# Whole-row gathers in three buffers, products three points later, and blocks of u turned in place, in a decoder layer with a product-key expert layer

## The chip, the cores and the metric

One core of a Trainium2 chip runs the whole layer as one program. The metric is the device time of one execution in microseconds (us). The median of three runs of the kernel before is 3408.37 us (3407.45 to 3411.59).

## What is computed

The reference is one decoder layer over 512 tokens of width 2048, in float32: a modulation from `c`, a projection, a short gated convolution beside differential attention, an output projection, and then a product-key expert layer (PEER). The change lies in that last part:

```python
s1 = jnp.einsum('thd,nd->thn', q[:, :, 0], keys1)      # 8 heads, 128 keys of each half
s2 = jnp.einsum('thd,nd->thn', q[:, :, 1], keys2)
...                                                    # 16 of the 128 x 128 experts per token and head: idx, g
u = jnp.take(expert_u, ib, axis=0)
a = jnp.einsum('thkd,td->thk', u, xb)
w = (jax.nn.gelu(a.astype(jnp.float32), approximate=False) * gb).astype(xb.dtype)
vv = jnp.take(expert_v, ib, axis=0)
return jnp.einsum('thk,thkd->td', w, vv)
```

Each token picks 8 x 16 = 128 of 16384 experts; each expert is a row of 2048 numbers in `expert_u` and one in `expert_v`.

## The kernel before

The kernel is written in a tile language. Its functions emit instructions in program order; a scheduler then gives each engine one fixed order, by simulated times and by dependencies, and no engine leaves that order on the chip. A tile of a pool with `bufs=n` has n buffers, and a new tile waits until an old buffer is free. A dependency called ORDER shapes that order alone; one called SYNC makes the instruction wait on the chip.

**Two ways for the experts.** The first TG = 160 tokens are *gathered*, the other TD = 352 are *dense*. For the dense tokens all 128 blocks of 128 experts are multiplied: `u_block(e)` (L796) makes 48 matmuls of u for a block (L804), a Gelu follows, `w_block(e)` (L829) multiplies by the gates, and `v_group(ch, dg)` (L945) makes the matmuls of v (L960) for a chunk of CH = 8 blocks and a quarter of the columns: 4 steps of 24 matmuls. TensorE works on float32 split into two parts (`split`, L87: ScalarE copies the first part at L88, VectorE subtracts it at L89), three passes for each product.

**Blocks of u.** A block of u must be turned. It lies in `u_dram` in an order in which VectorE's transposes of 32 x 32 finish the turn. `u_turn(n)` (L781) brings half a block: SP loads `ur` (L787, two buffers, a whole block), VectorE transposes one half into `utf` (L792, two buffers), and `split` makes `ut` from it (two buffers). The first NPRE = 12 blocks are turned ahead in `u_ahead` (L533), while TensorE does the output projection: `uar` is loaded, four transposes (L530) write `uat`, and SP stores that in `u_dram`.

**Gathered tokens.** Their rows of u and v come by indirect DMAs that GpSimd issues (`gathered`, L856), half a row (1024 numbers) for each of 128 partitions, into `gt`, four buffers. `gather_u` (L865) multiplies the half row with the token on VectorE and sums it (L867); after all of them `gather_w` applies Gelu and gate; `gather_v` (L876) adds the half row times its weight to `gacc` (L883). Group 0 are 128 tokens with 128 experts each; the other 32 tokens are folded into 32 columns (`gather_next` reloads tokens, indices and gates). That makes 160 x 2 x 2 = 640 gathers and 643 steps.

**Pace.** `pace` collects matmuls: every 12th of a u block, and the last of each 24 in a v group. After each, `gather_to` (L902) emits as many steps as belong there, so that all are emitted at the end of chunk 14; each gather waits (SYNC) for the latest matmul in `pace`, and its product stands right behind it in the program. Blocks 0 to 11 run before the gathers begin.

**Other users of `gt`.** Before that, the four score tiles `held` (L824) and the one-hot tiles `oh` (L920, 88 of them, VectorE at L921), from which TensorE (L930) makes the gate table `g_dram`, take the same four buffers.

**The end.** In the last chunk, `add_gathered(dg)` (L990) transposes the gathered tokens' sums: `ar` from `a_dram` (group 0, L999) and `gacc` (L1003). `store(dg)` (L1011) transposes the result into `ot` (four buffers) and writes it.

Of the kernel before, what the change touches and what calls it, by code (L numbers as in the profile page):

```python
# [39 lines left out]
GBUF = 4  # L40
# [12 lines left out]
PU_BUFS = 1  # L53
# [5 lines left out]
UTF_BUFS = 2  # L59
# [19 lines left out]
def hymba_peer(tc, x, c, positions, w_ada, b_ada, norm1_g, w_in, conv_w, q_norm_g, k_norm_g,  # L79
# [18 lines left out]
    with ExitStack() as ctx:  # L98
# [430 lines left out]
        def u_quarter(t, ur, q):  # L529
            nc.vector.transpose(t, ur[:, :, q * P:(q + 1) * P].rearrange("p b (c r) -> p c b r", r=32))  # L530


        def u_ahead(e):  # L533
            ur = pu.tile([P, 4, 512], F32, name="uar")
            u_load(ur, e)
            t = pu.tile([P, 4, 4, 4, 32], F32, name="uat", bufs=PU_BUFS)
            for q in range(4):
                u_quarter(t[:, q], ur, q)
            nc.sync.dma_start(u_dram[e], t.rearrange("p q c b r -> p (q c b r)"))
# [241 lines left out]
        def u_turn(n):  # L781
            e, q = divmod(n, 2)
            if e >= NK:
                return
            if q == 0:
                UR[0] = up.tile([P, 4, 512], F32, name="ur", bufs=UR_BUFS)
                nc.sync.dma_start(UR[0].rearrange("p b d -> p (b d)"), u_dram[e])  # L787
            if e < NPRE:
                t = UR[0][:, 2 * q:2 * q + 2].rearrange("p a (c b r) -> p (a c) b r", c=4, b=4)
            else:  # L790
                t = up.tile([P, 8, 4, 32], F32, name="utf", bufs=UTF_BUFS)
                nc.vector.transpose(t, UR[0][:, :, q * 256:(q + 1) * 256].rearrange("p b (c r) -> p c b r", r=32))  # L792
            UT[n] = up.tile([P, 2, 8, P], F32R, name="ut", bufs=UT_BUFS)
            split(UT[n], t.rearrange("p c b r -> p c (b r)"))

        def u_block(e, behind=None):  # L796
            pa = psA.tile([P, T], F32, name="pa")
            for q in range(2):
                u_turn(e * 2 + q + AHEAD)
                ut = UT.pop(e * 2 + q)  # L800
                for j in range(8):
                    k = q * 8 + j
                    for n, (a, b) in enumerate(PASSES):
                        mm = nc.tensor.matmul(pa[:, :TD], ut[:, a, j], hd[k][:, b],  # L804
                                              start=(k == 0 and n == 0), stop=(k == KC - 1 and n == 2))
# [18 lines left out]
        held = [scores(qs, i, psV.tile([P, T], F32, name="pv"), gp.tile([P, D // 2], F32, name="gt", bufs=GBUF)[:, 0:T])  # L824
# [29 lines left out]
        ga_a = gp.tile([P, 2, P], F32, name="ga_a")  # L854

        def gathered(src, g, j, f):  # L856
            t = gp.tile([P, D // 2], F32, name="gt", bufs=GBUF)
            d = nc.gpsimd.indirect_dma_start(out=t, out_offset=None, in_=src,  # L858
                                             in_offset=bass.IndirectOffsetOnAxis(ap=gidx[g][:, j:j + 1], axis=0),
                                             element_offset=f * (D // 2))  # L860
# [4 lines left out]
        def gather_u(g, j, f):  # L865
            t = gathered(expert_u, g, j, f)
            nc.vector.scalar_tensor_tensor(t, t, 1.0, h2n[:, f * D // 2:(f + 1) * D // 2], op0=OP.mult, op1=OP.mult,  # L867
                                           accum_out=ga_a[:, f, j:j + 1])

        def gather_w(g, w):  # L870
            a = ga_a[:, 0, :w]
            nc.vector.tensor_tensor(out=a, in0=a, in1=ga_a[:, 1, :w], op=OP.add)
# [3 lines left out]
        def gather_v(g, j, f):  # L876
            t = gathered(expert_v, g, j, f)
            a = ga_a[:, 0, j:j + 1]
            s = slice(f * D // 2, (f + 1) * D // 2)
            if j == 0:  # L880
                nc.vector.tensor_scalar(gacc[:, s], t, a, None, op0=OP.mult)
            else:
                nc.vector.scalar_tensor_tensor(gacc[:, s], t, a, gacc[:, s], op0=OP.mult, op1=OP.add)  # L883
# [10 lines left out]
        for g in range(NG):  # L894
            w = P if g == 0 else P // fold
            if g:
                steps.append((gather_next, ()))
            steps += [(gather_u, (g, j, f)) for j in range(w) for f in range(2)] + [(gather_w, (g, w))] + \
                     [(gather_v, (g, j, f)) for j in range(w) for f in range(2)]
        done = [0]  # L900

        def gather_to(blocks):  # L902
            first = 0.55 * CH
            frac = min(1.0, max(0.0, (blocks - first) / (NK - first - CH)))
            while done[0] < math.ceil(len(steps) * frac):
                f, a = steps[done[0]]
                f(*a)
                done[0] += 1


        with tc.tile_pool(name="gs", bufs=2, side="right") as gs:
# [78 lines left out]
        def add_gathered(dg):  # L990
            if NG == 2:
                ar = fin.tile([P, 512], F32, name="ar")
# [77 lines left out]
```

## Time and profile before

| what | value |
|---|---|
| median of three runs | 3408.37 us |
| the profiled execution's own time | 3427.17 us |
| its span, first to last instruction | 3424.9 us |
| TensorE matmuls busy | 3189.8 us (93%) |
| VectorE busy | 2840.9 us (83%) |
| ScalarE busy | 1219.8 us (36%) |
| GpSimd busy | 1419.2 us (41%) |
| DMA, mean rate | 297 GB/s |
| granted TensorE clock, mean share of full speed | 0.972 |

The engines are PE (TensorE; PEld its weight loads), DVE (VectorE), ACT (ScalarE), POOL (GpSimd) and SP (SyncE, which issues most DMAs). A row names a line of the kernel, an engine and an operation; `out<-in` are the program's tile names. "Idle before" is what the engine stood still just before such instructions, and the arrow names what ended that. Matmuls are pipelined, so that the durations of single ones overlap; a count in a stretch says more than their busy time.

### The profile page before, as it was taken

To read this page: it belongs to the slowest core of one execution; us is meant where nothing else is said; L and a number is where in the kernel's file an instruction comes from. 1 tells how busy PE (TensorE), PEld (TensorE's weight loads), DVE (VectorE), ACT (ScalarE), POOL (GpSimd) and SP (SyncE) were. 2 spreads that over 40 slices of the span, in tenths; PEclk is the share of its full clock that TensorE was granted. 3 is DMA by queue.
4 is the path that set the end of the run, shared out by engine and by line. 5 is a ranking of instruction groups with operands and counts; after the bars stand their busy time and mean duration, and the time that the engine had idled before them with its cause. 6 is when DMAs were issued, how large, how long until landed. Compare 5 with 4: busy or idle time off the path is not lost.

```text
span 3424.9 us, 48472 instructions
## 1 busy us (share of the span) xinstructions
PE 3189.8 (93%) x18006; PEld 2950.5 (86%) x18006; DVE 2840.9 (83%) x4261; ACT 1219.8 (36%) x1826; POOL 1419.2 (41%) x985
## 2 busy tenths in 40 slices
PE   5888999999998869899999999999999999999986
PEld 4666877777877659899899999999999999999985
DVE  5789667842339999889999999989999999999885
ACT  5232344343254437632333332323333333233322
POOL 2446423354436620034454444454444444445441
PEclk9998999999999979999999999999999999999997
DMA  8885978967999789989989999999889898999984
GB/s 292 261 261 173 318 246 279 301 229 223 308 299 299 229 276 342 328 296 340 320 322 334 317 324 315 318 315 336 317 316 333 305 334 317 326 327 331 322 285 174
DMA packets 434987, 1017.92 MB, mean 297 GB/s; under 512 B 34833, under 2 KB 113598, under 8 KB 415166
## 3 DMA queue, kind: packets, MB, share of 16 engines
q1 hardware_dynamic: 342590, 679.23, 58.7%
q0 software_dynamic: 92160, 335.59, 27.4%
q8 instruction: 141, 2.31, 0.3%
q14 instruction: 96, 0.79, 0.1%
HBM read 965.11 MB, written 171.18 MB: 332 GB/s over the span
## 4 chain that ended last, share of the span: by engine, by line
PE 39%; DVE 15%; DMA 11%; issue 6%; POOL 2%; ACT 0%; SPq 0%; DVEq 0%; ACTq 0%; POOLq 0%
PE pa L804 18%; PE pv L960 18%; DMA gt<-in_expert_u_dram,idxu 5%; DVE gt L867 2%; DMA gt<-in_expert_v_dram,ib 2%; PE pv L930 2%; DMA u_dram<-in_expert_u_dram 2%; DVE vs L89 1%; DVE utf L792 1%; DVE ut L89 1%; DVE gt L921 1%; DVE gacc L883 1%; POOL gt L858 1%; DVE tkj L691 1%; PE pm L561 1%
## 5 line engine op out<-in xcount | busy, mean ns | idle before, releaser
L804 PE MATMUL pa<-hd,ut 128*128 128x352 f32 x6144 | 1078.3, 327 | 41.9 <-DVE ut L89 32.3
L960 PE MATMUL pv<-W,vs 128*128 128x352 f32 x6144 | 1058.2, 325 | 20.6 <-ACT W L88 10.1
L804 PEld LDWEIGHTS pa<-hd,ut 128*128 128x128 f32 x6144 | 1010.2, 190 | 48.1 <-DVE ut L89 36.6
L960 PEld LDWEIGHTS pv<-W,vs 128*128 128x128 f32 x6144 | 1004.0, 189 | 26.9 <-ACT W L88 11.9
L89 POOL TENSOR_TENSOR wsp<-wraw,wsp 128x1024 fp32r<-128x1024 f32 x160 | 393.2, 2460 | 546.4 <-ACT wsp L88 519.4
L858 POOL DMA_INDIRECT gt<-in_expert_u_dram,idxu x256 | 347.4, 1357 | 593.8 <-DVE gt L867 239.0
L858 POOL DMA_INDIRECT gt<-in_expert_v_dram,idxu x256 | 342.4, 1337 | 434.9 <-DVE gacc L883 282.5
L88 ACT ACTIVATE vs<-vr 128x1024 fp32r<-128x1024 f32 x256 | 271.4, 1060 | 693.0 <-PE pv L960 635.6
L867 DVE SCALAR_TENSOR_TENSOR gt<-gt,h2n 128x1024 f32<-128x1024 f32 x320 | 384.3, 1217 | 68.7 <-DMA gt<-in_expert_u_dram,idxu 60.4
L883 DVE SCALAR_TENSOR_TENSOR gacc<-gt,ga_a,gacc 128x1024 f32<-128x1024 f32 x316 | 397.8, 1277 | 41.9 <-DMA gt<-in_expert_v_dram,ib 22.6
L88 ACT ACTIVATE ut<-utf 128x1024 fp32r<-128x1024 f32 x232 | 245.2, 1057 | 298.2 <-PE pa L804 184.5
L89 DVE TENSOR_TENSOR vs<-vr,vs 128x1024 fp32r<-128x1024 f32 x256 | 309.7, 1211 | 31.3 <-ACT vs L88 31.3
L88 ACT ACTIVATE wsp<-wraw 128x1024 fp32r<-128x1024 f32 x160 | 169.1, 1058 | 383.8 <-issue 99.7
L89 DVE TENSOR_TENSOR ut<-utf,ut 128x1024 fp32r<-128x1024 f32 x232 | 282.2, 1219 | 22.7 <-ACT ut L88 22.3
L792 DVE STREAM_TRANSPOSE utf<-ur 128x1024 f32<-128x1024 f32 x232 | 287.2, 1240 | 0.1
L471 PE MATMUL pm<-big,wsp 128*128 128x512 f32 x1152 | 284.6, 400 | 0.0
L471 PEld LDWEIGHTS pm<-big,wsp 128*128 128x128 f32 x1152 | 213.9, 190 | 42.4 <-issue 0.2
L196 DVE SCALAR_TENSOR_TENSOR ada_acc<-ada_w,scol,ada_acc 128x512 f32<-128x512 f32 x195 | 201.1, 1031 | 42.5 <-DMA ada_w<-in_w_ada_dram 38.8
L257 PE MATMUL pqk<-wsp,big 128*128 128x512 f32 x768 | 192.4, 409 | 24.7 <-DVE qk L303 17.8
L716 PE MATMUL pm<-big,wsp 128*128 128x512 f32 x768 | 188.8, 404 | 17.0 <-POOL wsp L89 15.4
L257 PEld LDWEIGHTS pqk<-wsp,big 128*128 128x128 f32 x768 | 149.2, 197 | 61.6 <-DVE qk L303 21.5
L716 PEld LDWEIGHTS pm<-big,wsp 128*128 128x128 f32 x768 | 147.1, 195 | 50.1 <-POOL wsp L89 18.0
(274 smaller groups left out, 3197.9 us busy)
## 6 DMA issues: line engine op xcount, KB each, us to landing
ur<-u_dram SPq DMA_DIRECT2D x128, 1024.0 KB, 7.7
vr<-in_expert_v_dram SPq DMA_DIRECT2D x256, 512.0 KB, 6.8
u_dram<-in_expert_u_dram SPq DMA_DIRECT2D x464, 256.0 KB, 6.7
ada_w<-in_w_ada_dram SPq DMA_DIRECT2D x192, 512.0 KB, 5.3
wraw<-in_w_in_dram SPq DMA_DIRECT2D x96, 512.0 KB, 5.9
g_dram<-gtile SPq DMA_DIRECT2D x11, 2048.0 KB, 7.4
g<-g_dram SPq DMA_DIRECT2D x32, 704.0 KB, 9.3
wraw<-in_w_out_dram SPq DMA_DIRECT2D x32, 512.0 KB, 5.5
```

The costliest lines, as they stand in the source:

```text
L88: hi = nc.scalar.activation(dst[:, 0], src, AF.Copy)
L89: (eng or nc.vector).tensor_tensor(out=dst[:, 1], in0=src, in1=dst[:, 0].bitcast(F32), op=OP.subtract)
L196: nc.vector.scalar_tensor_tensor(new, wt[:, k], s, old, op0=OP.mult, op1=OP.add)
L257: nc.tensor.matmul(banks[i], hT[kk][:, a, i * P:(i + 1) * P], ws[:, b, k], start=(kk == last[0] and n == 0), stop=(kk == last[1] and n == 2))
L471: nc.tensor.matmul(banks[n2], ws[:, a, k, n2 * P:(n2 + 1) * P], hT[kk][:, b], start=(kk == 0 and n == 0), stop=(kk == KC - 1 and n == 2))
L716: nc.tensor.matmul(banks[j], ws[:, a, k, j * P:(j + 1) * P], h2T[kk][:, b], start=(kk == 0 and n == 0), stop=(kk == KC - 1 and n == 2))
L792: nc.vector.transpose(t, UR[0][:, :, q * 256:(q + 1) * 256].rearrange("p b (c r) -> p c b r", r=32))
L804: mm = nc.tensor.matmul(pa[:, :TD], ut[:, a, j], hd[k][:, b], start=(k == 0 and n == 0), stop=(k == KC - 1 and n == 2))
L858: d = nc.gpsimd.indirect_dma_start(out=t, out_offset=None, in_=src, in_offset=bass.IndirectOffsetOnAxis(ap=gidx[g][:, j:j + 1], axis=0), e ...
L867: nc.vector.scalar_tensor_tensor(t, t, 1.0, h2n[:, f * D // 2:(f + 1) * D // 2], op0=OP.mult, op1=OP.mult, accum_out=ga_a[:, f, j:j + 1])
L883: nc.vector.scalar_tensor_tensor(gacc[:, s], t, a, gacc[:, s], op0=OP.mult, op1=OP.add)
L960: mm = nc.tensor.matmul(pv[j // 2][:, j % 2, :TD], vs[:, a, bb, j * P:(j + 1) * P], W[e0 // 2][:, m, bb], start=(b == 0 and n == 0), stop= ...
```

## The change

Gathers bring whole rows (2048 numbers), so 320 gathers and 323 steps; `gt` has three buffers of twice the size, and so have the users beside the gathers: `held` needs four of three, and `oh` takes half of one. A product is no longer emitted behind its gather but kept in `held_back` and emitted when `pace` has grown by LAG = 3, or when three are held, or before `gather_w`, `gather_next` and the end. `u_turn` transposes a half of `ur` in place, `utf` is gone, and the split reads `ur` in runs of 32. `u_ahead` transposes `uar` in place, with three buffers, and stores it. `ar` takes a buffer of `ot` instead of two of its own.

```diff
-GBUF = 4
+GBUF = 3
+LAG = 3
-PU_BUFS = 1
+PU_BUFS = 3
-UTF_BUFS = 2
...
         def u_ahead(e):
-            ur = pu.tile([P, 4, 512], F32, name="uar")
+            ur = pu.tile([P, 4, 512], F32, name="uar", bufs=PU_BUFS)
             u_load(ur, e)
-            t = pu.tile([P, 4, 4, 4, 32], F32, name="uat", bufs=PU_BUFS)
-            for q in range(4):
-                u_quarter(t[:, q], ur, q)
-            nc.sync.dma_start(u_dram[e], t.rearrange("p q c b r -> p (q c b r)"))
+            for b in range(4):
+                nc.vector.transpose(ur[:, b], ur[:, b])
+            nc.sync.dma_start(u_dram[e], ur.rearrange("p b d -> p (b d)"))
...
-            if e < NPRE:
-                t = UR[0][:, 2 * q:2 * q + 2].rearrange("p a (c b r) -> p (a c) b r", c=4, b=4)
-            else:
-                t = up.tile([P, 8, 4, 32], F32, name="utf", bufs=UTF_BUFS)
-                nc.vector.transpose(t, UR[0][:, :, q * 256:(q + 1) * 256].rearrange("p b (c r) -> p c b r", r=32))
-            UT[n] = up.tile([P, 2, 8, P], F32R, name="ut", bufs=UT_BUFS)
-            split(UT[n], t.rearrange("p c b r -> p c (b r)"))
+            t = UR[0][:, :, q * 256:(q + 1) * 256]
+            if e >= NPRE:
+                nc.vector.transpose(t, t)
+            UT[n] = up.tile([P, 2, 8, 4, 32], F32R, name="ut", bufs=UT_BUFS)
+            split(UT[n], t.rearrange("p b (c r) -> p c b r", r=32))
...
-        def gathered(src, g, j, f):
-            t = gp.tile([P, D // 2], F32, name="gt", bufs=GBUF)
+        def gathered(src, g, j):
+            t = gp.tile([P, D], F32, name="gt", bufs=GBUF)
             d = nc.gpsimd.indirect_dma_start(out=t, out_offset=None, in_=src,
-                                             in_offset=bass.IndirectOffsetOnAxis(ap=gidx[g][:, j:j + 1], axis=0),
-                                             element_offset=f * (D // 2))
+                                             in_offset=bass.IndirectOffsetOnAxis(ap=gidx[g][:, j:j + 1], axis=0))
...
-        def gather_u(g, j, f):
-            t = gathered(expert_u, g, j, f)
-            nc.vector.scalar_tensor_tensor(t, t, 1.0, h2n[:, f * D // 2:(f + 1) * D // 2], op0=OP.mult, op1=OP.mult,
-                                           accum_out=ga_a[:, f, j:j + 1])
+        def gather_u(g, j):
+            t = gathered(expert_u, g, j)
+            return lambda: nc.vector.scalar_tensor_tensor(t, t, 1.0, h2n, op0=OP.mult, op1=OP.mult,
+                                                          accum_out=ga_a[:, j:j + 1])
...
+        def use_next():
+            i = held_back.pop(0)[1]()
+            if pace:
+                tc.add_manual_dep(i.ins, pace[-1].ins.name, ORDER, reason="rows have landed")
 
         def gather_to(blocks):
             first = 0.55 * CH
             frac = min(1.0, max(0.0, (blocks - first) / (NK - first - CH)))
+            while held_back and held_back[0][0] + LAG <= len(pace):
+                use_next()
             while done[0] < math.ceil(len(steps) * frac):
                 f, a = steps[done[0]]
-                f(*a)
+                while held_back and (len(held_back) == GBUF or f in (gather_w, gather_next)):
+                    use_next()
+                use = f(*a)
+                if use is not None:
+                    held_back.append((len(pace), use))
                 done[0] += 1
+            while held_back and frac == 1.0:
+                use_next()
...
-                    oh = gp.tile([P, D // 2], F32, name="gt", bufs=GBUF).rearrange("p (a t n) -> p a t n", a=2, n=P)
+                    oh = gp.tile([P, D], F32, name="gt", bufs=GBUF)[:, 0:D // 2].rearrange("p (a t n) -> p a t n", a=2, n=P)
...
-                ar = fin.tile([P, 512], F32, name="ar")
+                ar = fin.tile([P, T], F32, name="ot", bufs=4)
```

`gather_v` is changed as `gather_u` is, and `gather_w` no longer adds two half sums.

## Rows read from the trace of the kernel before

**Rows 1.** By stretches: start:end and length, busy us (count) of PE, PEld, DVE, ACT, POOL; clock, DMA share, GB/s.

```profile
1265.00:1380.00 115.00, 110.29 (x810) 109.44 (x809) 108.82 (x140) 86.75 (x200) 0.24 (x1) 0.97 0.90 324
...
1600.00:1720.00 120.00, 112.51 (x676) 110.75 (x676) 111.37 (x145) 35.39 (x40) 57.10 (x44) 0.97 0.91 321
...
1900.00:2320.00 420.00, 408.33 (x2493) 403.78 (x2493) 383.78 (x460) 128.38 (x144) 203.58 (x143) 0.99 0.91 318
2320.00:3000.00 680.00, 680.00 (x4227) 680.00 (x4226) 644.78 (x581) 214.94 (x242) 294.14 (x226) 1.00 0.90 323
...
3302.00:3425.00 123.00, 76.28 (x413) 70.92 (x411) 75.70 (x141) 23.82 (x54) 24.41 (x20) 0.79 0.59 209
```

**Rows 2.** Waits of TensorE, 1900 to 2320: total us, times, longest.

```profile
PE pa L804 <- DVE ut L89: 6.7, 7, 2.3
```

**Rows 3.** Waits of VectorE, 1900 to 2320.

```profile
DVE gt L867 <- DMA gt<-in_expert_u_dram,idxu: 27.2, 20, 2.8
```

**Rows 4.** Timeline of TensorE near the end: start, us, what, [idle before].

```profile
3365.32 0.69 PE L1003 MATMUL pa<-ident,gacc 128*128 128x128 f32 x2 [22.28 <-DVE gacc L883]
```

**Rows 5.** By stretches: L960 alone (PE, PEld; first, last row), L858 alone (POOL).

```profile
0.00:3271.80 3271.80, 982.51 (x5760) 933.83 (x5760) 0.98 0.88 301
...
1440.00:3271.80 1831.80, 826.15 (x610) 1.00 0.91 322
3271.80:3425.00 153.20, 37.74 (x30) 0.83 0.62 218
...
3302.00:3425.00 123.00, 63.69 (x316) 58.89 (x315) 0.79 0.59 209
```

**Rows 6.** Timeline of GpSimd: the first and the last of 640 gathers.

```profile
1450.99 1.38 POOL L858 DMA_INDIRECT gt<-in_expert_u_dram,idxu  x1 [183.56 <-DVE utf L792]
...
3361.09 1.50 POOL L858 DMA_INDIRECT gt<-in_expert_v_dram,ib  x1 [1.33 <-DVE gacc L883]
```

**Rows 7.** Waits over the whole span, GpSimd's gathers for products.

```profile
POOL gt L858 <- DVE gacc L883: 357.8, 173, 10.3
POOL gt L858 <- DVE gt L867: 322.0, 156, 6.2
```

**Rows 8.** DMA issues: count, KB each (none for indirect ones), median us to landing.

```profile
ur<-u_dram SPq DMA_DIRECT2D x128, 1024.0 KB, 7.7
vr<-in_expert_v_dram SPq DMA_DIRECT2D x256, 512.0 KB, 6.8
...
gt<-in_expert_u_dram,idxu POOLq DMA_INDIRECT x256, 7.0
...
ar<-a_dram SPq DMA_DIRECT2D x4, 256.0 KB, 11.2
```

**Rows 9.** Groups of instructions: count, busy us, mean ns, idle us before, what ended it.

```profile
L883 DVE SCALAR_TENSOR_TENSOR gacc<-gt,ga_a,gacc 128x1024 f32<-128x1024 f32 x316 | 397.8, 1277 | 41.9 <-DMA gt<-in_expert_v_dram,ib 22.6 <-DMA gt<-in_expert_v_dram,idxu 18.8
...
L867 DVE SCALAR_TENSOR_TENSOR gt<-gt,h2n 128x1024 f32<-128x1024 f32 x320 | 384.3, 1217 | 68.7 <-DMA gt<-in_expert_u_dram,idxu 60.4 <-DMA gt<-in_expert_u_dram,ib 8.1
...
L89 DVE TENSOR_TENSOR ut<-utf,ut 128x1024 fp32r<-128x1024 f32 x232 | 282.2, 1219 | 22.7 <-ACT ut L88 22.3
L88 ACT ACTIVATE vs<-vr 128x1024 fp32r<-128x1024 f32 x256 | 271.4, 1060 | 693.0 <-PE pv L960 635.6 <-issue 38.1 <-DMA vr<-in_expert_v_dram 10.6
...
L837 DVE TENSOR_TENSOR ge<-ge,g 128x704 f32<-128x704 f32 x58 | 51.5, 887 | 2.1 <-ACT ge L821 2.1
L89 DVE TENSOR_TENSOR W<-ge,W 128x704 fp32r<-128x704 f32 x58 | 51.4, 887 | 0.0
```

**Rows 10.** The DMA queue of the gathers: packets, MB, share of 16 engines.

```profile
q0 software_dynamic: 92160, 335.59, 27.4%
```

**Rows 11.** By stretches: L921 alone (DVE), then L930 alone (PE, PEld).

```profile
1265.00:1301.80 36.80, 21.45 (x18) 0.91 0.90 303
...
1265.00:1301.80 36.80, 17.74 (x120) 17.30 (x121) 0.91 0.90 303
```

**Rows 12.** Waits of SP, whole span.

```profile
SPq L787 <- DVE utf L792: 512.8, 112, 12.1
```

More of the change, by code (lines that the diff above doesn't have):

```diff
@@ L527, in u_load @@
                                       .rearrange("(b r) d -> r b d", r=32))
-        def u_quarter(t, ur, q):
-            nc.vector.transpose(t, ur[:, :, q * P:(q + 1) * P].rearrange("p b (c r) -> p c b r", r=32))
         def u_ahead(e):
-            ur = pu.tile([P, 4, 512], F32, name="uar")
+            ur = pu.tile([P, 4, 512], F32, name="uar", bufs=PU_BUFS)
             u_load(ur, e)
-            t = pu.tile([P, 4, 4, 4, 32], F32, name="uat", bufs=PU_BUFS)
-            for q in range(4):
-                u_quarter(t[:, q], ur, q)
-            nc.sync.dma_start(u_dram[e], t.rearrange("p q c b r -> p (q c b r)"))
+            for b in range(4):
+                nc.vector.transpose(ur[:, b], ur[:, b])
+            nc.sync.dma_start(u_dram[e], ur.rearrange("p b d -> p (b d)"))
         ahead = list(range(NPRE))
@@ L803, in u_block @@
                     for n, (a, b) in enumerate(PASSES):
-                        mm = nc.tensor.matmul(pa[:, :TD], ut[:, a, j], hd[k][:, b],
+                        mm = nc.tensor.matmul(pa[:, :TD], ut[:, a, j].rearrange("p b r -> p (b r)"), hd[k][:, b],
                                               start=(k == 0 and n == 0), stop=(k == KC - 1 and n == 2))
@@ L822, in u_block @@
             return mm
-        held = [scores(qs, i, psV.tile([P, T], F32, name="pv"), gp.tile([P, D // 2], F32, name="gt", bufs=GBUF)[:, 0:T])
+        held = [scores(qs, i, psV.tile([P, T], F32, name="pv"), gp.tile([P, D], F32, name="gt", bufs=GBUF)[:, 0:T])
                 for i in range(NT)]
@@ L853, in hymba_peer @@
             ggate.append(gb_)
-        ga_a = gp.tile([P, 2, P], F32, name="ga_a")
-        def gathered(src, g, j, f):
-            t = gp.tile([P, D // 2], F32, name="gt", bufs=GBUF)
+        ga_a = gp.tile([P, P], F32, name="ga_a")
+        def gathered(src, g, j):
+            t = gp.tile([P, D], F32, name="gt", bufs=GBUF)
             d = nc.gpsimd.indirect_dma_start(out=t, out_offset=None, in_=src,
-                                             in_offset=bass.IndirectOffsetOnAxis(ap=gidx[g][:, j:j + 1], axis=0),
-                                             element_offset=f * (D // 2))
+                                             in_offset=bass.IndirectOffsetOnAxis(ap=gidx[g][:, j:j + 1], axis=0))
             if pace:
@@ L863, in gathered, with gather_v @@
             return t
-        def gather_u(g, j, f):
-            t = gathered(expert_u, g, j, f)
-            nc.vector.scalar_tensor_tensor(t, t, 1.0, h2n[:, f * D // 2:(f + 1) * D // 2], op0=OP.mult, op1=OP.mult,
-                                           accum_out=ga_a[:, f, j:j + 1])
+        def gather_u(g, j):
+            t = gathered(expert_u, g, j)
+            return lambda: nc.vector.scalar_tensor_tensor(t, t, 1.0, h2n, op0=OP.mult, op1=OP.mult,
+                                                          accum_out=ga_a[:, j:j + 1])
         def gather_w(g, w):
-            a = ga_a[:, 0, :w]
-            nc.vector.tensor_tensor(out=a, in0=a, in1=ga_a[:, 1, :w], op=OP.add)
+            a = ga_a[:, :w]
             nc.scalar.activation(a, a, AF.Gelu)
             nc.vector.tensor_tensor(out=a, in0=a, in1=ggate[g], op=OP.mult)
[L876 to L879, printed above, removed]
+        def gather_v(g, j):
+            t = gathered(expert_v, g, j)
+            a = ga_a[:, j:j + 1]
             if j == 0:
-                nc.vector.tensor_scalar(gacc[:, s], t, a, None, op0=OP.mult)
-            else:
-                nc.vector.scalar_tensor_tensor(gacc[:, s], t, a, gacc[:, s], op0=OP.mult, op1=OP.add)
+                return lambda: nc.vector.tensor_scalar(gacc, t, a, None, op0=OP.mult)
+            return lambda: nc.vector.scalar_tensor_tensor(gacc, t, a, gacc, op0=OP.mult, op1=OP.add)
         def gather_next():
@@ L897, in hymba_peer @@
                 steps.append((gather_next, ()))
-            steps += [(gather_u, (g, j, f)) for j in range(w) for f in range(2)] + [(gather_w, (g, w))] + \
-                     [(gather_v, (g, j, f)) for j in range(w) for f in range(2)]
+            steps += [(gather_u, (g, j)) for j in range(w)] + [(gather_w, (g, w))] + [(gather_v, (g, j)) for j in range(w)]
         done = [0]
+        held_back = []
+        def use_next():
+            i = held_back.pop(0)[1]()
+            if pace:
+                tc.add_manual_dep(i.ins, pace[-1].ins.name, ORDER, reason="rows have landed")
         def gather_to(blocks):
```

## The prediction

> **What bounds the kernel now.** I read the table by stretches first [rows 1]. From 2320 to 3000 us TensorE is busy all 680.0 us and issues 4227 matmuls, 680.0 / 4227 = 0.161 us each: that is the full rate, and nothing on another engine can gain there. Against it, 1600 to 1720 has 676 matmuls, worth 676 x 0.161 = 108.8 us of 120, so 11.2 us are lost; 1900 to 2320 has 2493, worth 401.4 of 420, so 18.6 are lost. Both lie where rows of u are gathered. The waits of TensorE in the second name the VectorE split of `ut` [rows 2], and in the same stretch VectorE stands still 27.2 us, in 20 waits, because the row that its next product needs has not landed [rows 3]. VectorE works in order, so the splits stand behind that product.
>
> The last stretch, 3302 to 3425, has 413 matmuls in 123 us and a granted clock of 0.79 [rows 1], that is partly the lower of the two levels (1.2 and 2.4 GHz). The reader should look for one line in its timeline: TensorE stands 22.28 us before a transpose of `gacc`, until a product has made it [rows 4]. Why is `gacc` late? Not for the pace: all 5760 matmuls of the v groups of chunks 0 to 14 (15 x 16 x 24), behind which the last gathers are put, are issued by 3271.8, and 30 gathers still go out afterwards [rows 5]. The first starts at 1450.99, the last at 3361.09 [rows 6]: 1910.1 / 639 = 2.99 us per half row. GpSimd waits mostly for products to free a buffer, 357.8 and 322.0 us [rows 7]. So the stream of gathers is held by its four buffers: one goes round in 4 x 2.99 = 11.96 us, of which 7.0 are issue to landing [rows 8] and 1.25 the product [rows 9]; the other 3.7 are waiting for VectorE and for GpSimd.
>
> **The change part by part.**
>
> *Products.* The VectorE sums of L89 take 887 ns for 704 elements (`W`) and 1219 for 1024 (`ut`) [rows 9], so an element costs 332 / 320 = 1.04 ns and 1024 more cost 1062. A whole row then takes 1217 + 1062 = 2279 (u) and 1277 + 1062 = 2339 (v). A u row saves 2434 - 2279 = 155 ns and one read of the accumulator, a v row 2554 - 2339 = 215; 160 of each save 59 us of VectorE. The other end, a row costing just twice a half, saves 0. I take 59, as the rows are of this engine and kind. In the full stretches this lies beside TensorE and is worth nothing by itself.
>
> *Gathers.* GpSimd's 640 issues are 826.2 + 37.7 = 863.9 us [rows 5]; 320 take 432 if an issue costs per instruction, 864 if per byte, and both are under half of the 1985 us. Landing of 1 MB is not shown for this queue. The nearest rows are `ur` and `vr`: 1024 KB land in 7.7 us, 512 KB in 6.8 [rows 8], so 0.9 more, 7.9; the other end is twice 7.0, 14.0. I take 7.9, since those rows share the same DMA engines. Three buffers: 7.9 + 2.3 + 3.7 = 13.9 us round, 4.6 us per row where 2 x 2.99 = 5.98 is used now; the stream then gains on its pace and ends with it, near 3271.8 + 13.9 + 2.3 = 3288, before the last u block at 3302. At 14.0 it is 20.0 round, 6.7 per row, and it falls behind (a rival below).
> A rule speaks against the larger rows. The rows: all of the gathers' packets take 27.4% of 16 engines [rows 10], 0.274 x 16 x 3424.9 / 92160 = 0.163 us each, and ScalarE's copies of `vr` wait only 10.6 us for its DMA [rows 9]; by them the sum stands as it is. The Trainium skill ("DMA: Bandwidth & Descriptors", Queues, rings and completion order) says that a DMA engine turns from queue to queue packet by packet. By that rule an estimate is that a `vr` load of 16 turns per engine lands up to 16 x 0.163 = 2.6 us later. If ScalarE's 10.6 us tripled and all reached TensorE, the sum would lose 21.
>
> *Products three points behind.* A point is 12 matmuls (1.9 us) in a u block and 24 (3.9 us) in a v group, and the two alternate; three points are at least 5.8 us. VectorE's waits for landings, 68.7 and 41.9 us in all [rows 9], should mostly go; what is late next is the product, which only GpSimd awaits. Behind those waits stood the splits, and of the 11.2 + 18.6 = 29.8 us lost I take 21 back, by bounds of 10 and 30: some are TensorE's own order of u and v.
>
> *Tail.* 3302 to 3425 holds 316 matmuls of v, 50.9 us at the full rate where they took 63.69 [rows 5], and 97 others, 76.28 - 63.69 = 12.6 us [rows 1, 5]; with the some 12 us of last copies and stores behind the last v matmul, 76 of 123. So 47 is the most to be had. I take 25: the 22.28 us wait and a little of the clock, and leave the splits and loads as they are. Against it, `ar` now shares four buffers with the output tiles; its load takes 11.2 us [rows 8], and one such wait is the lower bound, 25 - 11 = 14.
>
> *Three buffers for the one-hot tiles.* At 1301.8 VectorE has begun 18 and TensorE has done 120 / 8 = 15 [rows 11]: three are in work, and the fourth buffer is being written next. With three, VectorE waits. TensorE has u blocks to put in (110.29 of 115 us busy [rows 1]). Bounds: 0, and one tile's 1.2 us for each four of the first 60, 18 us. I take 3. The four score tiles in three buffers delay only a copy of the last one: 0, covered by VectorE's selections.
>
> *Turning in place.* As many transposes of as many elements: 0. The split now reads runs of 32; L837 reads such runs of `g` in 887 ns, as long as L89's 704 elements without runs [rows 9]: 0. `ur` is freed by the split instead of the transpose. SP already waits for that buffer 512.8 us in 112 loads [rows 12], and `vr` loads stand behind it on SP. A block comes about every 31 / 2 = 15.5 us (96 matmuls of u and v x 0.161), so two buffers give 31; the load 7.7, a transpose taken as long as a split, a copy like that of `vs` and two splits (1.2 + 1.1 + 2.4) [rows 9] and half a block's distance, 7.8, make 20.2. Hidden, 0; 10 if not. The twelve blocks turned ahead get a third buffer under TensorE's matmuls: 0.
>
> Sum: -21 - 25 + 3 = -43 us. The profiled execution took 3427.17, 18.8 above the median shown, so 3427.17 goes to 3384.2, a ratio of 0.9875, and the median of 3408.37 to 3366.
>
> **The rivals.**
> - *Half of it* (crowded loads by the rule above, or the tail keeps a wait for `ar`): -22, 3386. For it: DMA is 0.9 busy in the full stretches [rows 1]. Against: ScalarE's 10.6 us.
> - *No gain*: VectorE's order is fixed before the run, and buffers that fill force products before the three points; the waits come back as they are. 3408, within 0.2% (6.8 us, about what a measurement can tell from no change).
> - *Slower by the landing.* A row that takes over 17.9 - 2.3 - 3.7 = 11.9 us to land makes three buffers slower than four halves. At 12.5 us it is 0.2 us per row, 320 x 0.2 = 64 us later at `gacc`: 3472. Against: the `ur` row's 7.7.
> - *Slower by the one-hot buffers*: 18 lost there and 10 by `ur`, with nothing regained: 3436. It decides where TensorE has no u block ready.
> - *The change doesn't do what it says*: if the stream never catches its pace, three points change nothing; that is the no-gain case.
>
> **How the numbers follow.** Forecast 0.60 (own range 3336 to 3384), half 0.17, no gain 0.09, slower by landing 0.07, by buffers 0.07. Faster by over 0.2%: 0.77; within: 0.09; slower: 0.14. A range of 3336 to 3414 holds the forecast but for its upper end of gain, the half and the no-gain case, and leaves out both slower ones.
>
> **What would show it.** Right: 320 gathers, products near 2.28 and 2.34 us; VectorE's waits for landings under 40 us; near 746 matmuls in any 120 us from 1600 on; the last product before the last u block, and no wait of over 5 us before L1003's transposes. Wrong: landing over 12 us; TensorE waiting for the one-hot tiles; more than 10 gathers after the last v matmul of chunk 14; new waits for `ut` or `vs`.

## The result, and the profile after

| | before | after |
|---|---|---|
| median | 3409.98 us (3407.45 to 3413.76) | 3386.86 us (3382.44 to 3396.71) |
| the profiled execution's own time | 3427.17 us | 3396.71 us |
| its span | 3424.9 us | 3394.6 us |

The ratio is 0.9932 [0.9915, 0.995], in brackets the 95% interval: faster by 0.7%, inside the range, but by 23 us and not by 43. The two profiled executions, each slower than its kernel's median (by 17 and 10 us), differ by 30.3 us of span. Where these lie is read from the first and the last matmul of a line in TensorE's timeline; the stretches of both kernels are then as long as in this table. "Main loop" is from the first u matmul of block 12 to the last u matmul, and the tail goes from there to the end.

| stretch | before | after | difference | predicted |
|---|---|---|---|---|
| up to the first matmul of the output projection | 766.1 | 771.0 | +4.9 | none |
| output projection (L561 before, L557 after) | 192.1 | 200.0 | +7.8 | 0 |
| from there to the first gate-table matmul | 314.4 | 314.5 | +0.1 | 0 |
| gate table from one-hot tiles (L930, L933) | 153.2 | 168.6 | +15.4 | +3 |
| main loop | 1868.6 | 1848.2 | -20.5 | -21 |
| tail | 122.8 | 84.9 | -38.0 | -25 |

The first row is no effect of the change: no line that it touches runs there, and in all fourteen profiles this point lies anywhere from 757.7 to 771.0.

The table by stretches of the kernel after has the columns of [rows 1]:

```profile
1600.00:1720.00 120.00, 115.91 (x700) 115.04 (x700) 113.41 (x106) 36.11 (x41) 28.99 (x23) 0.97 0.90 345
1900.00:2320.00 420.00, 419.82 (x2607) 419.51 (x2606) 392.09 (x345) 134.11 (x152) 112.60 (x76) 1.00 0.91 338
2320.00:3000.00 680.00, 678.21 (x4205) 676.49 (x4205) 646.36 (x487) 215.82 (x242) 162.48 (x121) 1.00 0.90 335
...
3309.80:3394.60 84.80, 69.25 (x419) 64.19 (x417) 48.43 (x118) 23.34 (x54) 0.00 (x0) 0.93 0.49 168
```

From 1900 to 2320 TensorE now issues 2607 matmuls where [rows 1] had 2493, which is the full rate (420 / 0.161 = 2608). From 1600 to 1720 it issues 700 where the prediction wanted near 746, so 7 of the 120 us are still lost there (11 before). The last line is the tail: idle time of TensorE there has gone from 46.7 us (123 - 76.28) to 15.6, and the granted clock has risen from 0.79 to 0.93.

Groups of instructions after, with the columns of [rows 9]:

```profile
L873 DVE SCALAR_TENSOR_TENSOR gacc<-gt,ga_a,gacc 128x2048 f32<-128x2048 f32 x158 | 369.5, 2339 | 3.0 <-DMA gt<-in_expert_v_dram,idxu 2.2 <-DMA gt<-in_expert_v_dram,ib 0.8
L860 DVE SCALAR_TENSOR_TENSOR gt<-gt,h2n 128x2048 f32<-128x2048 f32 x160 | 364.3, 2281 | 14.9 <-DMA gt<-in_expert_u_dram,idxu 14.9
...
L852 POOL DMA_INDIRECT gt<-in_expert_u_dram,idxu x128 | 181.7, 1419 | 724.4 <-DVE gt L860 318.8 <-DVE W L831 197.4 <-PE pv L963 153.5
L852 POOL DMA_INDIRECT gt<-in_expert_v_dram,idxu x128 | 175.2, 1369 | 551.1 <-DVE gacc L873 382.1 <-PE pv L963 73.1 <-issue 36.3
```

A whole row's product takes 2281 and 2339 ns (2279 and 2339 were expected), an issue costs per instruction (1419 and 1369 ns for twice the bytes), and VectorE's idle time before products is 14.9 + 3.0 = 17.9 us where it was 68.7 + 41.9 [rows 9]. Over the whole span GpSimd's gathers wait 312 us for matmuls, that is for the pace itself (`pv` 271.7, `pa` 40.4), where they waited 172 (93.3 and 78.3): the stream now keeps up with it.

How the stream ends, first GpSimd's last gather, then VectorE's last product, then the first transpose of `gacc` on TensorE, from their timelines:

```profile
3274.56 0.94 POOL L852 DMA_INDIRECT gt<-in_expert_v_dram,ib  x1 [9.40 <-PE pv L963]
...
3286.58 2.34 DVE L873 SCALAR_TENSOR_TENSOR gacc<-gt,ga_a,gacc 128x2048 f32<-128x2048 f32 x1
...
3320.55 0.50 PE L1006 MATMUL pa<-ident,gacc 128*128 128x128 f32 x2
```

The last gather waited for a matmul of v and not for a buffer; the last product ends at 3288.9, 21 us before the last u matmul (3309.8), and the transpose, which had 22.28 us of idle time before it [rows 4], now has none.

What the change costs shows in the waits of the gate-table stretch (1285 to 1455) and of the output projection (771 to 971), both of the kernel after, with the columns of [rows 2]:

```profile
PE pv L933 <- DVE og L927: 21.9, 29, 3.2
...
DVE gt L924 <- PE pv L933: 11.2, 16, 1.2
```

```profile
ACT wsp L88 <- DMA wraw<-in_w_out_dram: 39.7, 7, 14.8
...
PE pm L557 <- ACT wsp L88: 6.3, 1, 6.3
```

In the first VectorE waits 11.2 us for TensorE to give a one-hot buffer back, and TensorE 21.9 us for `og`, which VectorE makes from a one-hot tile. In the second TensorE waits for a part of the weights of the output projection, as their load (`wraw`) came late.

### The profile page after: what moved, and what is told of

It is laid out like the page before. It is cut to its first block, busy times and chain, and to the rows that moved or that the text cites. A ratio compares the mean times of both kernels' runs of the same rounds, so it can differ in the third digit from the quotient of the medians.

```text
span 3394.6 us, 47070 instructions
## 1 busy us (share of the span) xinstructions
PE 3183.8 (94%) x18006; PEld 2947.5 (87%) x18006; DVE 2815.8 (83%) x3779; ACT 1218.1 (36%) x1826; POOL 1002.0 (30%) x665
## 4 chain that ended last, share of the span: by engine, by line
PE 68%; DVE 17%; DMA 9%; issue 2%; ACT 1%; SPq 1%; POOL 1%; DVEq 0%; ACTq 0%; POOLq 0%
PE pv L963 27%; PE pa L798 27%; DMA ada_w<-in_w_ada_dram 5%; PE pm L471 5%; DVE ada_acc L196 2%; PE pm L557 2%; DVE run L196 2%; DVE gt L924 2%; PE pm L257 2%; PE pm L712 1%; DMA wraw<-in_w_out_dram 1%; PE pv L933 1%; DVE tkj L687 1%; PE sp L425 1%; DVE cv L674 1%
## 5 line engine op out<-in xcount | busy, mean ns | idle before, releaser
L798 PE MATMUL pa<-hd,ut 128*128 128x352 f32 x6144 | 1066.7, 326 | 28.7 <-DVE ut L89 21.7
L852 POOL DMA_INDIRECT gt<-in_expert_u_dram,idxu x128 | 181.7, 1419 | 724.4 <-DVE gt L860 318.8
L860 DVE SCALAR_TENSOR_TENSOR gt<-gt,h2n 128x2048 f32<-128x2048 f32 x160 | 364.3, 2281 | 14.9 <-DMA gt<-in_expert_u_dram,idxu 14.9
L88 ACT ACTIVATE ut<-ur 128x1024 fp32r<-128x1024 f32 x256 | 269.5, 1055 | 296.6 <-PE pa L798 229.5
L873 DVE SCALAR_TENSOR_TENSOR gacc<-gt,ga_a,gacc 128x2048 f32<-128x2048 f32 x158 | 369.5, 2339 | 3.0 <-DMA gt<-in_expert_v_dram,idxu 2.2
L89 DVE TENSOR_TENSOR ut<-ur,ut 128x1024 fp32r<-128x1024 f32 x256 | 310.4, 1216 | 46.8 <-ACT ut L88 45.9
L852 POOL DMA_INDIRECT gt<-in_expert_v_dram,idxu x128 | 175.2, 1369 | 551.1 <-DVE gacc L873 382.1
L786 DVE STREAM_TRANSPOSE ur<-ur 128x1024 f32<-128x1024 f32 x232 | 274.4, 1219 | 10.6 <-DMA ur<-u_dram 10.6
L196 DVE SCALAR_TENSOR_TENSOR ada_acc<-ada_w,scol,ada_acc 128x512 f32<-128x512 f32 x195 | 208.1, 1067 | 39.0 <-DMA ada_w<-in_w_ada_dram 35.0
L712 PE MATMUL pm<-big,wsp 128*128 128x512 f32 x768 | 187.3, 401 | 19.5 <-POOL wsp L89 17.9
```

Of the source, the lines that this page charges most:

```text
L88: hi = nc.scalar.activation(dst[:, 0], src, AF.Copy)
L89: (eng or nc.vector).tensor_tensor(out=dst[:, 1], in0=src, in1=dst[:, 0].bitcast(F32), op=OP.subtract)
L196: nc.vector.scalar_tensor_tensor(new, wt[:, k], s, old, op0=OP.mult, op1=OP.add)
L712: nc.tensor.matmul(banks[j], ws[:, a, k, j * P:(j + 1) * P], h2T[kk][:, b], start=(kk == 0 and n == 0), stop=(kk == KC - 1 and n == 2))
L786: nc.vector.transpose(t, t)
L798: mm = nc.tensor.matmul(pa[:, :TD], ut[:, a, j].rearrange("p b r -> p (b r)"), hd[k][:, b], start=(k == 0 and n == 0), stop=(k == KC - 1 a ...
```

## The experiments

Each time is a median; behind it stands the ratio to the kernel before on the same chip. Stretches come from one profile of each kernel. One theory, *bytes*, says that the gain comes from 24 KB of gather buffers per partition (three whole rows) in place of 16 (four halves), which turning in place pays for; its rival, *order*, that it comes from the products three points later, behind which the splits no longer stand.

**E1: two one-hot tiles in each buffer.** The kernel after, with

```diff
-                    oh = gp.tile([P, D], F32, name="gt", bufs=GBUF)[:, 0:D // 2].rearrange(...)
+                    s4 = b * (GB // 4) + t4 // 4
+                    if s4 % 2 == 0:
+                        pair = gp.tile([P, D], F32, name="gt", bufs=GBUF)
+                    oh = pair[:, (s4 % 2) * (D // 2):(s4 % 2 + 1) * (D // 2)].rearrange(...)
```

> The changed kernel, with two one-hot tiles in each of the three buffers, so six at a time instead of three. The one-hot stretch (first to last matmul of the gate table) is 1272.6 to 1425.9 = 153.3 us before and 1285.4 to 1454.0 = 168.6 after. Theory A (three buffers made VectorE wait there): back to 152 to 158 us, and the time 10 to 15 us under that of the changed kernel, near 0.989 of before. Theory B (another order of the scheduler, not the buffers): it stays at 165 to 172, and the time within 4 us of the changed kernel, near 0.993.

Measured: 3381.49 us, 0.9918 [0.9903, 0.9932]. The gate table takes 158.9 us in place of 168.6, and VectorE's wait for a free one-hot buffer is gone from its list. E2 and E3, which keep three, are at 166.6 and 166.4. So some 8 to 10 of the 15.4 us are the lack of one-hot buffers, as stretches show it; the intervals of the whole time overlap.

**E2: the blocks ahead not in place.** The kernel after, with two buffers of `uar` and a tile of its own for the transposes:

```diff
-            ur = pu.tile([P, 4, 512], F32, name="uar", bufs=PU_BUFS)
+            ur = pu.tile([P, 4, 512], F32, name="uar")
+            t = pu.tile([P, 4, 512], F32, name="uat", bufs=1)
...
-                nc.vector.transpose(ur[:, b], ur[:, b])
+                nc.vector.transpose(t[:, b], ur[:, b])
...
```

> The changed kernel, with the twelve blocks turned ahead into a tile of their own again (two buffers of uar, one of uat), the rest as changed. The output projection's matmuls run from 766.1 to 958.3 = 192.2 us before and from 771.0 to 971.0 = 200.0 after. Theory A (turning ahead in place costs the 7.8): back to 190 to 194, the time 5 to 8 us lower. Theory B (it only varies from run to run, or comes from elsewhere): 198 to 202, the time within 3 us of the changed kernel.

Measured: 3374.35 us, 0.9902 [0.9887, 0.9916]. The output projection is back at 192.1 us, and neither ScalarE's wait for `wraw` nor TensorE's 6.3 us is in that stretch any more. So the loss was there because the weights came late, and SP's order shows why: ahead of the twelfth load of `wraw` it issues 40 loads of `uar` in the kernel after and 24 in E2, as in the kernel before, and that load goes out 70.8 us behind the stretch's first matmul after, 54.6 in E2. Which part does it, the third buffer or turning in place, stays open: the run undoes both.

**E3: products at once.** The kernel after, with `use()` where a product was put into `held_back`.

> The changed kernel with each product right behind its gather, as before the change, whole rows and three buffers kept. From the first matmul of block 12 to the last of u it takes 1433.4 to 3302.1 = 1868.7 us before and 1461.6 to 3309.8 = 1848.2 after. Theory A (the three points give the 20 us, as they take VectorE's waits for landings away): those waits rise from 17.9 us to over 60, the stretch goes back to 1862 to 1872, and the end after u stays near 85 us, as whole rows keep the stream on its pace: time 15 to 22 us over the changed kernel. Theory C (whole rows alone do it, by less VectorE time): the stretch stays within 1844 to 1853 and the time within 5 us.

Measured: 3378.87 us, 0.9909 [0.9893, 0.9924]; main loop 1843.0 us, tail 85.5. Without the three points nothing of the gain is lost, though VectorE's idle time before products rises from 17.9 to 26 us. From the start of a gather to the start of its product are 13.22 us in the mean of all 320 here, and 13.26 after: the lag hardly moved a product. That a product has its place in VectorE's fixed order and waits there is the likely reason; no run shows it by itself.

**E4: the kernel before once more**, for a second profile of it.

> The kernel before once more, unchanged, to see how far two profiles of one kernel differ. The output projection's first matmul comes at 766.1 us before and 771.0 after, ahead of every changed instruction. All theories: if it moves by some 5 us here too, that part of the shift is no effect of the change; and the stretches 192.2 (output projection), 153.3 (one-hot), 1868.7 (block 12 to the end of u) and 122.8 (from there to the end) should come again within 3 us.

Measured: 3412.51 us in one run. Main loop 1862.6 us and tail 117.4, against 1868.6 and 122.8: single stretches vary by some 6 us from profile to profile, more than the 3 expected.

**E9: three points alone.** The kernel before, half rows and four buffers, with `held_back` and LAG = 3 of the kernel after and nothing else.

> The kernel before with the three points alone: half rows, four buffers, utf, each product emitted three points behind its gather. Theory A's step on the prediction's record (late products take VectorE's waits away): its waits for landings fall from 110 us to under 50, and block 12 to the end of u from 1865 to under 1855. Theory W (they change nothing while buffers bind): waits 90 to 120, the stretch 1860 to 1872, the end after u 115 to 125, time within 5 us of before.

Measured: 3414.47 us, 1.0008 [0.999, 1.0027]: no change that can be measured. VectorE's idle time before products falls from 110.6 to 86.8 us. The main loop takes 1857.1 us, under the 1868.6 and 1862.6 of the two profiles before, but E14 below, with no lag, has 1857.9; the tail is 123.7. The theory *order* falls with E3 and E9.

**E6: two buffers of whole rows**, that is 16 KB, products at once, with the pairs of E1.

```diff
-GBUF = 3
-LAG = 3
+GBUF = 2
+LAG = 0
```

> The changed kernel with whole rows, products at once, but two buffers instead of three, as many bytes as before; one-hot tiles in pairs, so four of them as before. Theory W: the stream falls behind its pace as before or more, over 25 gathers of whole rows are left when the last v matmul of chunk 14 is issued, the stretch from block 12 to the end of u is over 1862 and the end after u over 115, time 3405 or more. Theory X: under 1853 and under 95, time 3378 to 3388.

Measured: 3510.24 us, 1.03 [1.0277, 1.0323]. Its DMA issues (columns as [rows 8]) and its first transpose of `gacc`:

```profile
gt<-in_expert_u_dram,idxu POOLq DMA_INDIRECT x128, 8.3
gt<-in_expert_v_dram,idxu POOLq DMA_INDIRECT x128, 8.2
```

```profile
3450.18 0.69 PE L1009 MATMUL pa<-ident,gacc 128*128 128x128 f32 x2 [47.52 <-DVE gacc L873]
```

A whole row lands in 8.2 to 8.3 us (medians). A buffer goes round in 12.33 us (first to last gather, divided by 319, times two), 6.16 us per row, where three buffers let the stream keep its pace at 5.63 (after), and TensorE stands 47.52 us for `gacc`. At this row size 16 KB instead of 24 cost 4%.

**E7: turning in place alone.** The kernel before with four buffers of half rows, `u_turn` and `u_ahead` of the kernel after.

> The kernel before with the turns in place alone: four half-row buffers, products at once, u_ahead in place with three buffers, no utf. All theories: output projection 198 to 202 us (192.2 before), as in every run that turns ahead in place; the end after u 115 to 125, since the gathers are as before. Theory A: one-hot stretch 152 to 155, as its four buffers are back, and block 12 to the end of u 1860 to 1870; time 4 to 10 us over before. Rival D (turning in place costs the rest of the one-hot stretch, 158.9 with six tiles in pairs, and gains in the main loop): one-hot 157 to 160, main loop 1845 to 1855.

Measured: 3459.58 us, 1.0152 [1.0131, 1.0173]. This is the largest surprise: a part that was costed at nothing costs some 52 us (0.0152 x 3412). The output projection takes 201.3 us (192.1 before), the gate table 157.7 (153.2), the main loop 1881.5, and the wait for `gacc` at the end is longer than the one in [rows 4]:

```profile
PE pa L996 <- DVE gacc L876: 30.8, 1, 30.8
```

**E5: six buffers of half rows.** E7 with GBUF = 6 (24 KB) and `ar` in `ot`; 640 gathers, products at once.

> The changed kernel with half rows again, 640 gathers, each product right behind its gather, but six buffers of half a row, as many bytes as three whole rows. Before (four half rows) the stretch from block 12 to the end of u is 1868.6 us and 1862.6 in its second profile, the end after u 122.8 and 117.4; with whole rows at once 1843.0 and 85.5. Theory W (the bytes that the buffers hold give the gain): 1843 to 1852 and 83 to 92, VectorE's waits for landings under 40 us, time within 6 us of 3379. Theory X (whole rows give it, by 59 us less of VectorE): the stretch stays over 1857 or the end over 105, time over 3392. One-hot stretch, with six buffers: 152 to 156.

Measured: 3390.82 us, 0.994 [0.9923, 0.9956]. Against E7 the main loop is 22.7 us shorter (1858.8), the tail 34.3 (91.8), and VectorE's idle time before products falls from 134.4 to 49.0 us. With six tiles the gate table takes 151.3 us, no longer than before. From E5 to E3 the rows become whole: main loop 1843.0, tail 85.5, 15.8 and 6.3 us less, but 15.1 more for the gate table with its three buffers. In this order the runs lead from the kernel before to the kernel after, one part at a time:

| kernel | what is added | ratio | output projection | gate table | main loop | tail |
|---|---|---|---|---|---|---|
| before | | 1 | 192.1 | 153.2 | 1868.6 | 122.8 |
| E7 | turning in place | 1.0152 | 201.3 | 157.7 | 1881.5 | 126.1 |
| E5 | 24 KB in six half rows | 0.9940 | 200.4 | 151.3 | 1858.8 | 91.8 |
| E3 | the same 24 KB in three whole rows | 0.9909 | 199.8 | 166.4 | 1843.0 | 85.5 |
| after | products three points later | 0.9932 | 200.0 | 168.6 | 1848.2 | 84.9 |

So the bytes carry most of the gain, and whole rows add 22 us of stretches, of which the one-hot tiles take 15 back; the ratios of E5 and E3 just touch in their intervals. Bytes are not all: 16 KB as two whole rows (E6, 1.03) are slower than as four halves (E7).

**E8: the three edits that helped**, E1, E2 and E3 together in the kernel after.

> The changed kernel with the three edits that each gained by itself: two one-hot tiles per buffer, blocks ahead turned out of place, products right behind their gathers. If the losses that they take away lie in separate stretches (one-hot 10 us, output projection 8, main loop 2 to 5), the output projection takes 192 us, the gate table 157 to 159, the main loop 1843 to 1846, and the time is about 3360 to 3368, 0.986 of the kernel before. If TensorE would have waited for something else in those stretches in any case (work is only moved from one to the next), it is no faster than the best of the three, 3374.

Measured: 3367.92 us (3363.95 to 3377.52), 0.9873 [0.985, 0.9896], the fastest of the study. Output projection 191.2 us, gate table 157.1, main loop 1843.3: the losses were separate and nearly add up (by the ratios E1, E2 and E3 gained 5, 10 and 8 us over the kernel after, and E8 gained 20).

**Why turning in place costs, E10, E14, E13.** E10 is E7 with a third buffer of `ur`:

```diff
-UR_BUFS = 2
+UR_BUFS = 3
```

> The kernel before with the blocks turned in place, and a third buffer for ur. Theory: turning in place costs time in the main loop since ur is held until the split and so loads of ur start later (half a block's buffer less in the chain); then a third buffer brings the main loop from 1881 back to 1860 to 1868, and the time to about 3425, the 9 us of the output projection staying. Rival: the order that the scheduler fixes, or the transposes in place themselves, cost it; then the main loop stays near 1880 and the time near 3455.

Measured: 3465.94 us, 1.0151 [1.0129, 1.0173], main loop 1880.0. Nothing comes back; that `ur` has too few buffers is not the cause. The theory that I had for E10 falls.

E14 is the kernel before with only the order of a turned block changed, in `u_turn` and `u_ahead`, so that the split reads runs of 32; all tiles are kept:

```diff
-                t = up.tile([P, 8, 4, 32], F32, name="utf", bufs=UTF_BUFS)
-                nc.vector.transpose(t, UR[0][:, :, q * 256:(q + 1) * 256].rearrange("p b (c r) -> p c b r", r=32))
...
+                f = up.tile([P, 4, 256], F32, name="utf", bufs=2)
+                nc.vector.transpose(f, t)
+                t = f
```

> The kernel before, all tiles and buffers kept; the transposes only write blocks in the order that the changed kernel has, and so the split reads runs of 32. If reading in runs costs time (the splits or their order), the main loop goes from 1869 to about 1881 and the time by 10 to 20 us up. If turning in place itself is what costs, this is within 0.2% of the kernel before.

Measured: 3403.16 us against 3401.76, 1.0001 [0.9989, 1.0013]. Reading in runs is free, as predicted.

E13 is E14 with one edit more, `nc.vector.transpose(t, t)` in place of the tile `utf`:

> The same, with u_turn in place and utf gone; the blocks turned ahead still go through a tile of their own. If turning in place in the main loop is what costs, the main loop is at 1880 to 1890 and the output projection back at 192: about 3445 to 3450, 1.010 to 1.013 of the kernel before. If only the blocks ahead cost, it is within 0.3% of the kernel before.

Measured: 3445.49 us, 1.0127 [1.0107, 1.0147]; output projection 191.5, main loop 1881.2 (E14: 1857.9), tail 141.2 (115.7). So `u_turn` in place costs some 43 us by itself (0.0127 x 3402), and `u_ahead` the 9 or so that E7 has above that. The difference is to be seen in VectorE's timeline. First E14, the two transposes of one block and the first of the next (lines between left out):

```profile
2504.43 1.24 DVE L787 STREAM_TRANSPOSE utf<-ur 128x1024 f32<-128x1024 f32 x1
...
2519.41 1.24 DVE L787 STREAM_TRANSPOSE utf<-ur 128x1024 f32<-128x1024 f32 x1
...
2522.87 1.24 DVE L787 STREAM_TRANSPOSE utf<-ur 128x1024 f32<-128x1024 f32 x1
```

Then E13:

```profile
2502.24 1.28 DVE L877 SCALAR_TENSOR_TENSOR gacc<-gt,ga_a,gacc 128x1024 f32<-128x1024 f32 x1 [0.98 <-DMA gt<-in_expert_v_dram,idxu]
2503.44 2.37 DVE L786 STREAM_TRANSPOSE ur<-ur 128x1024 f32<-128x1024 f32 x2
2505.73 1.24 DVE L877 SCALAR_TENSOR_TENSOR gacc<-gt,ga_a,gacc 128x1024 f32<-128x1024 f32 x1
...
2518.18 1.29 DVE L877 SCALAR_TENSOR_TENSOR gacc<-gt,ga_a,gacc 128x1024 f32<-128x1024 f32 x1 [1.09 <-DMA gt<-in_expert_v_dram,idxu]
2519.38 1.22 DVE L88 TENSOR_TENSOR vs<-vr,vs 128x1024 fp32r<-128x1024 f32 x1
2520.52 2.37 DVE L786 STREAM_TRANSPOSE ur<-ur 128x1024 f32<-128x1024 f32 x2
```

"x2" in one line is two instructions without a pause. Over the 116 blocks the pause between the two transposes of a block is 7.49 us in the mean in E14, and the two run back to back in E13 (also in E7, E10 and the kernel after). With `utf`, the second transpose needs one of two buffers, which a split must have freed, and the scheduler's order spreads the transposes. In place it needs nothing that the first did not need, and it stands right behind the first. The stream then runs slower: first to last gather takes 1940.4 us in E13 and 1893.6 in E14, 3.04 and 2.96 us per half row, 47 us in all, which is about what the time shows.

Where in a buffer's round this lies, the traces tell in part. The traces of E13 and E14 hold no landings, but those of the kernel before and of E7 do: the round is 11.96 and 12.08 us in the mean, of which 7.04 and 7.27 are issue to landing (1.35 and 1.41 the issue itself), 2.71 and 2.65 the wait of a landed row for its product, 1.24 the product, and 0.98 and 0.92 the time until the next issue. So products do not stand longer behind the pairs; issue and landing take longer. For the issue a way is seen: beside a transpose it takes 0.94 us and beside a product or a split mostly more (last section), and 105 of 640 issues start during a transpose in E14 but 52 in E13; all issues sum to 867.9 and 911.8 us. Why the landing takes longer stays open. VectorE's transposes also wait for loads of `ur`, 15.8 us in E13, 11.6 in E7 and 24.0 in E10, against 0.1 us of idle time in E14.

E5's transposes are paired as well, and there, with six buffers, the main loop is no longer than in the kernel before. That the order is different, and that the loop of four buffers is slower, is shown; that the pairs cause it is inferred, since no run kept the transposes in place and pushed the second one half a block back. That was not tried.

## Why the prediction was right, and where not

**What bounds the kernel** was read rightly: losses where rows of u are gathered, and a stream of gathers that its buffers hold and that makes `gacc` late. More buffers of one row size make it faster (E7 to E5), fewer make it slower (E3 to E6). One reading was of a wider stretch than it says: the 27.2 us in 20 waits of [rows 3] are of 1880 to 2320; from 1900 on they are 25.0 in 19.

**The step "products three points behind"** failed: its size came right by luck (-21 predicted, -20.5 measured for the main loop), and its cause was wrong. By the table of parts the main loop went +12.9 by turning in place, -22.7 by the bytes, -15.8 by whole rows and +5.2 by the three points, which is within what two profiles of one kernel differ. The waits for landings went (17.9 us are left, under 40 as I wrote), but they go with deeper buffers; the lag alone changes nothing that can be measured (E9), and taking it away costs nothing (E3). The inference at fault was that the splits stand behind VectorE's waits, and so TensorE gains as these go: E9 took 24 us of them away for no gain that can be measured.

**Whole rows, landing and loop.** Products and issues were right to a few ns and a few per cent: the 320 issues sum to 444 us in four groups, 432 were expected. The landing was put at 7.9 us and is 8.2 to 8.3 where it could be read (E6, with two buffers); the far end of 14.0, and with it the rival of slower landings, is out. The free loop of 13.9 us can't be read off, since the stream waits for its pace now (16.9 us a round); the end of the last product, expected near 3288, came at 3288.9, but by luck, as the stretches before the main loop had by then taken 28 us more.

**Tail**: 25 was too little; 38. I had counted the wait for `gacc` and a little of the clock, and left splits and loads as they are. TensorE's other idle time there fell too, 46.7 - 15.6 = 31.1 us in all with the 22.3, while VectorE has 48.43 us to do in the tail and not 75.70 [rows 1]; and the matmuls of v, 323 now, take 58.12 us where 316 took 63.69 [rows 5], at a granted clock of 0.93 and not 0.79. `ar` in the buffers of `ot` cost no wait over 1.1 us. The line of v matmuls alone in the tail, by stretches (PE, PEld, clock, DMA share, GB/s):

```profile
3309.80:3394.60 84.80, 58.12 (x323) 53.27 (x321) 0.93 0.49 168
```

**Three buffers for the one-hot tiles**: +3 was mis-sized; +15.4, near the upper bound of 18. E1 gives 8 to 10 of it back. Of the rest a part is likely turning in place: with four one-hot tiles, as before, E7, E10 and E13 take 157.7, 158.9 and 155.1 us. That TensorE had u blocks to put in did not cover it: it waits 21.9 us for `og`, and 11.5 in the same stretch before, the sign of being wrong that the prediction named.

**Turning in place**: 0, with a bound of 10, was the step that failed most. Two reasons that I checked hold: runs of 32 are free (E14), and transposes in place are no slower (1219 ns after, 1240 before). The third, that `ur` has time enough, holds only as far as a third buffer gains nothing (E10); waits for its loads are new. What I left out is that a buffer is also an order: without `utf` the scheduler puts both transposes of a block together, and at four half-row buffers turning a block in place costs 1.27% (E13). With 24 KB of buffers the stream keeps its pace and TensorE its full rate from 1900 to 2320 all the same; how much of the cost is left there is not shown, since no run has 24 KB and keeps `utf`.

**Blocks turned ahead**: 0, covered by TensorE's matmuls, was wrong by 8 us; the cover is TensorE's own weights, and their load was the one that came late (E2).

**The rule of the Trainium skill.** ScalarE's copies of `vr` waited 10.6 us for its DMA before, and a loss of up to 21 us was worked out if that tripled. The waits for it in the kernel after, and then in E6, which has whole rows too:

```profile
ACT vs L88 <- DMA vr<-in_expert_v_dram: 6.1, 1, 6.1
```

```profile
ACT vs L88 <- DMA vr<-in_expert_v_dram: 18.6, 6, 3.6
```

The Trainium skill ("DMA: Bandwidth & Descriptors", Queues, rings and completion order) says that a DMA engine serves its queues in turn, packet by packet. With whole rows the loads of the other queue did not land later: `vr` and `ur` take 6.2 and 7.7 us in E6 (medians), and 6.8 and 7.7 before [rows 8]. So the longer wait in E6 does not come from later landings, and the larger rows cost nothing here that can be read as that rule. The 10.6 us that VectorE's transposes wait for `ur` in the kernel after are new, but half rows turned in place have them too (E7, 11.6).

So the sum missed by the small costs: 3 + 0 were expected for gate table and projection, and 15.4 + 7.8 came; the tail gave 13 us of that back. The time fell on the rival *half of it* (3386), but not by its reasons; E8, which takes most of these costs away, and the three points with them, is at 3367.92, near the forecast of 3366.

## What to carry to other kernels

Ask of a stream of loads how much its buffers hold before asking how late its consumer is put: here the lag took 24 us of waits from an engine with slack and gained nothing (E9). A tile that is saved is also a dependency that is lost, and where a scheduler fixes the order, its removal reorders the engine; read the order of the instructions after such an edit, as its cost can be hidden by another part of the same change. When one size serves several users (here the gathers, score and one-hot tiles), try to split the buffer for the small users; E1 did so.

## What was not expected of the hardware

The same unchanged work before the first changed instruction took 757.7 to 771.0 us in the fourteen profiles, so a stretch is only compared by its own length.

How long the issue of a gather takes on GpSimd depends on what VectorE is doing when it starts. In the kernel before, 103 of the 640 issues start during a transpose and 21 beside an idle VectorE, and each of these takes 0.94 us. 412 start during a product or a split's subtraction; these take 1.56 us in the mean, and 375 of them end 0.79 to 0.84 us after that instruction has ended, as if they had waited for it. One of each kind, from the timeline:

```profile
1955.55 1.24 DVE L792 STREAM_TRANSPOSE utf<-ur 128x1024 f32<-128x1024 f32 x1
1955.61 0.94 POOL L858 DMA_INDIRECT gt<-in_expert_u_dram,idxu  x1 [0.30 <-issue]
...
2506.83 1.22 DVE L89 TENSOR_TENSOR vs<-vr,vs 128x1024 fp32r<-128x1024 f32 x1
2506.88 1.98 POOL L858 DMA_INDIRECT gt<-in_expert_v_dram,idxu  x1 [3.23 <-DMA gt<-in_expert_v_dram,idxu]
```

The second issue ends at 2508.86, 0.81 us after the subtraction (2508.05). The other thirteen profiles show the same. All issues of the kernel before take 262 us more than 640 times 0.94; no run here shows what that costs the kernel.
